# Seven products for eight in six k-tiles: half of the last gating projection and half of the output projection of a decoder layer

## The chip, the core and the metric

The kernel runs on one core of one Trainium2 chip. A core has a matrix engine (TensorE, PE in the profile, with its weight loads as PEld), a vector engine (VectorE, DVE), a scalar engine (ScalarE, ACT), GpSimd (POOL), a queue that issues transfers (SyncE, SP), sixteen DMA engines, a working memory of 128 partitions (SBUF) and eight accumulation banks for the matrix engine (PSUM). Each engine works through its own queue of instructions; they wait for each other with semaphores. The metric is the time of one execution on the device, in microseconds; less is better. A time is the median of several executions.

## What is computed

One decoder layer for 256 tokens of width 2048. Three branches (a convolution module A, a gated spatial mixer B, sparse attention C) are computed from one normed input, each is projected to the model width and multiplied by a gate; the sum goes through the output projection and a norm, and then a feed-forward network follows. The part that matters here:

```python
h = rms_norm(x, norm_mix_pre[l])
proj = h @ w_in[l]
a_in, b_in, q, kv, nsa_g, merge_g = jnp.split(proj, splits, axis=-1)
y_a = conformer_conv(a_in, ...)             # ends in  h @ w_a_out
y_b = chunked_spatial_gating(b_in, ...)     # ends in  (u * f) @ w_b_out
y_c = native_sparse_attention(q, kv, ...)   # ends in  o @ w_c_out
g_a, g_b, g_c = jnp.split(jax.nn.sigmoid(merge_g), 3, axis=-1)
mixed = (g_a * y_a + g_b * y_b + g_c * y_c) @ w_o[l]
x = x + rms_norm(mixed, norm_mix_post[l])
```

The three gates are 3 x 2048 columns of `proj`. The gate of branch C is the last 2048 of them.

## The kernel before

**Numbers in two parts.** All large products are made in a shortened float32 format. Each operand is split into a high part and a rest (`whi`, `wlo` for weights; `hT[:, k, 0]` and `hT[:, k, 1]` for the input), and a product of 128x128 by 128x512 is made of three matmuls: high by high, high by rest, rest by high (`mm_t`, L191 to L194). Inputs are cut into k-tiles of 128 rows; 2048 rows are 16 k-tiles. Tokens come in two halves of 128 (`t` = 0, 1; H1 and H2 in the change), output columns in blocks of 512.

**Weights.** `fetch` issues a transfer of one weight piece (128x1024, 512 KB) into a ring of five buffers (`wraw`). ScalarE copies the high part into one of four `whi` buffers (L143), VectorE subtracts it for the rest into one of four `wlo` buffers (L144). A buffer of a ring is taken again when its last reader has finished; for `whi` and `wlo` the last reader is a matmul. `piece` (L129) does this for one piece, `granule` for two.

**PSUM.** Four banks form a ring called "acc", the other four a ring called "bg" (`bank`). A bank is taken again when its last reader has finished.

**The gating.** `branch(bi, act_of)` (L867) runs once per branch, and inside it over four blocks of 512 columns. For a block it makes the gate product `pg` from `hT` and `wt_g` over 16 k-tiles, in two banks (one per half of the tokens), takes tanh on ScalarE (L883, 128x256 each, four per block), makes the branch's own product `py` from its result (8 k-tiles) and `wt_p`, and then VectorE multiplies (L908) and adds into `mac` (L911). For branch C, `mix_gen` then transposes the four finished k-tiles of `mac` on TensorE (L921), writes the high part into `mh` (L922) and the rest into `ml` (L923).

**Work in the background.** `bg` is a list of generators; `pump` takes steps from it between the products, so that attention, sums and transposes lie among them. A planner then sets the order of the instructions on each engine by priorities; `tc.high_priority` raises them, and `tc.issue_after` and `in_line` fix an order.

**The output projection.** `mm_o` multiplies `mh`, `ml` with `wt_o` by blocks of 512 columns (cb), pairs of k-tiles (p) and halves of the tokens; `done_o` squares the result for the norm (L960) and multiplies it by the gain row `rw` (L962, tile rnmp). The last pieces are held back (`HELD`) so that the second half of the tokens can be interleaved with the next norm's transposes (`enter2`, L989).

**Seven for eight, already in use.** The down projection of the feed-forward network (`Pair`, L1236 on) takes its k-tiles in part by pairs. Two k-tiles, two halves of the tokens and two blocks of columns make eight products; with sums and differences of the activations and of the weights prepared beforehand, seven products and a few additions at the end give the same result (the scheme of Strassen and Winograd, with four of the products accumulated in banks of their own: p1, p5, p6, p7). `quad` prepares the weights of such a pair: four subtractions of 512 columns and the split of seven half-pieces, in an order fixed by `fixed`, where each instruction of VectorE or ScalarE follows the one before in its list (L980 is the line where all of these are issued). `combine` adds the side banks up at the end.

Of the kernel before, what the change touches and what calls it, by code (L numbers as in the profile page):

```python
# [23 lines left out]
R = mybir.dt.float32r  # L25
# [13 lines left out]
PLAIN = [*range(22, 33), 21, 10, *range(33, NFT)]  # L39
BA, BB, BC, BG = 2100, 2200, 2200, 2500  # L40
# [14 lines left out]
def block(ctx: ExitStack, tc: tile.TileContext, x, xf, fp, cst, rows, sgw, w1, w2, wf_a, wt_bv, wf_bu, wf_c,  # L55
          wt_vs, wf_q, wt_g, wt_p, wt_o, wf_up, wt_dn, wt_dq, out):
# [134 lines left out]
    def mm_t(ps, xh, xl, hi, lo, first, last):  # L191
        PE.matmul(ps, lhsT=xh, rhs=hi, start=first, stop=False)  # L192
        PE.matmul(ps, lhsT=xh, rhs=lo, start=False, stop=False)  # L193
        return PE.matmul(ps, lhsT=xl, rhs=hi, start=False, stop=last).ins  # L194
# [634 lines left out]

    def attn():  # L830
# [27 lines left out]


# [4 lines left out]
    def branch(bi, act_of):  # L864

        for cb in range(4):
# [20 lines left out]
            for q in range(2):  # L887
                hs = granule(wt_p[(bi * 4 + cb) * 2 + q])
                if cb == 0 and q == 0:
                    until("BAC"[bi])  # L890
                    if bi == 2:
                        mix["h"] = s16(P1, [128, KT, T], R, "mh")
                        mix["l"] = s16(P1, [128, KT, T], R, "ml")
                act = act_of()
                for k in range(4 * q, 4 * q + 4):
                    hi, lo = hs[(k % 4) // 2]
                    c = slice((k % 2) * 512, (k % 2) * 512 + 512)
                    for t in range(2):
                        ts = slice(t * 128, t * 128 + 128)
                        mm_t(py[t], act[:, k, 0, ts], act[:, k, 1, ts], hi[:, c], lo[:, c], k == 0, k == 7)  # L900
                if q == 0:
                    pump(BUDGET)
# [13 lines left out]
    def mix_gen(cb):  # L916

        for k in range(4 * cb, 4 * cb + 4):
            pt = bank([128, T], f"pm{k}")
            for t in range(2):  # L920
                PE.transpose(pt[:, t * 128:t * 128 + 128], mac[:, t, k * 128:k * 128 + 128], ident)  # L921
            S.activation(mix["h"][:, k], pt, AF.Copy, scale=0.5)  # L922
            V.scalar_tensor_tensor(mix["l"][:, k], pt, 0.5, mix["h"][:, k].bitcast(F32), op0=ALU.mult,  # L923
                                   op1=ALU.subtract)
            yield 500

# [4 lines left out]
    mh, ml = mix["h"], mix["l"]  # L931

# [12 lines left out]
    def wo(cb, p):  # L945
        return wt_o[cb * 4 + p // 2][:, (p % 2) * 1024:(p % 2) * 1024 + 1024]

    def mm_o(cb, t, p, hl, halves=(0, 1)):
        if p == 0 and 0 in halves:
            po[cb, t] = PS.tile([128, 512], F32, tag="acc", name=f"po{cb}_{t}")  # L950
# [21 lines left out]
    seq = {}  # L972

    def fixed(eng, op, *args, **kw):

        with ExitStack() as order:
            order.enter_context(tc.high_priority())
            for ins in seq.get(eng, ()):
                order.enter_context(tc.issue_after(ins))
            seq[eng] = [op(*args, **kw).ins]  # L980

    def order_of(last):
        seq[V] = seq[S] = list(last)

# [19 lines left out]
    for cb in range(3):  # L1004
        for p in range(8):
            if (cb, p) in HELD:
                continue
            hl = piece(wo(cb, p), 1024)
            for t in range(2):
                mm_o(cb, t, p, hl)  # L1010
            pump(1e6)
        if cb < 2:
            for t in range(2):
                done_o(cb, t)
# [146 lines left out]
    H1, H2 = slice(0, 128), slice(128, T)  # L1161

# [49 lines left out]

# [17 lines left out]
    def high(hi, x):  # L1230
        fixed(S, S.activation, hi, x, AF.Copy)

    def rest(lo, x, hi):
        fixed(V, V.tensor_sub, lo, x, hi.bitcast(F32))

    def weights(src, into=None):  # L1236
        raw = fetch(src, 1024)
        hi, lo = (into[:, 0], into[:, 1]) if into is not None else ring(raw.name)
        high(hi, raw)
        rest(lo, raw, hi)  # L1240
        return hi, lo

    def ring(name):
        return [P0.tile([128, 1024], R, tag=tag, bufs=4, name=f"{tag}{name}") for tag in ("whi", "wlo")]

    class Pair:
        def __init__(self, p):
            self.p = p
            main = [PS.tile([128, 512], F32, tag="acc", name=f"pd{p}a{i}") for i in range(4)]
            side = [bank([128, 512], f"pd{p}b{i}") for i in range(4)]  # L1250
            if not p:
                main, side = side, main
            self.c = [main[0:2], main[2:4]]
            self.p1, self.p5, self.p6, self.p7 = side
            self.begun, self.left = set(), {}

        def mm(self, bank, a, w, last=False):

            first = id(bank) not in self.begun
            self.begun.add(id(bank))  # L1260
            for j, (x, y) in enumerate(((0, 0), (0, 1), (1, 0))):
                ins = PE.matmul(bank, lhsT=a[x], rhs=w[y], start=first and j == 0, stop=last and j == 2).ins  # L1262
            return ins

        def plain(self, i):

            hi, lo = weights(wt_dn[self.p, i])
            for n in range(2):
                c = slice(n * 512, n * 512 + 512)
                for t in range(2):  # L1270
                    in_line(self.mm, self.c[t][n], g2(PLAIN[i], (H1, H2)[t]), (hi[:, c], lo[:, c]),
                            self.p == 0 and i == len(PLAIN) - 1)

        def quad(self, n):
# [3 lines left out]
            last = n == len(PAIRS) - 1  # L1278
            L, U = slice(0, 512), slice(512, 1024)
# [3 lines left out]
            nm = f"q{self.p}_{j}"  # L1283
            tt = scratch()
            (hb, lb), (ha, la), (ht, lt), (h4, l4) = (ring(nm + x) for x in "bat4")
            high(hb, b)
            fixed(V, V.tensor_sub, tt[:, L], b[:, L], a[:, U])
            fixed(V, V.tensor_sub, a[:, U], a[:, U], a[:, L])
            high(ha, a)
            rest(lb, b, hb)  # L1290
            fixed(V, V.tensor_sub, tt[:, U], b[:, L], a[:, U])
            high(ht, tt[:, 0:1024])
            rest(la, a, ha)
            fixed(V, V.tensor_sub, tt[:, 1024:], b[:, U], tt[:, U])
            high(h4[:, L], tt[:, 1024:])
            rest(lt, tt[:, 0:1024], ht)
            rest(l4[:, L], tt[:, 1024:], h4[:, L])
            src = (se, sf)[j // 5]
            s1, s2, s4 = ((src[:, 0, j % 5, i], src[:, 1, j % 5, i]) for i in range(3))
            for bank_, act, (h, l), c in (  # L1300
                    (self.c[0][1], s4, (hb, lb), L), (self.c[0][0], g2(k1, H1), (hb, lb), U),
                    (self.p1, g2(k0, H1), (ha, la), L), (self.p5, s1, (ha, la), U),
                    (self.p7, g2(k0, H2), (ht, lt), L), (self.p6, s2, (ht, lt), U),
                    (self.c[1][0], g2(k1, H2), (h4, l4), L)):
                side = any(bank_ is x for x in (self.p1, self.p5, self.p6, self.p7))
                in_line(self.mm, bank_, act, (h[:, c], l[:, c]), last and side)
# [4 lines left out]

        def combine(self):

            fixed(S, S.activation, self.at(0, 0), self.p1, AF.Copy)
            fixed(V, V.tensor_add, self.at(1, 0), self.p6, self.at(0, 0))
            fixed(V, V.tensor_add, self.at(0, 1), self.p5, self.at(1, 0))
            fixed(V, V.tensor_add, self.at(1, 1), self.p7, self.at(0, 1))
            fixed(V, V.tensor_add, self.at(1, 0), self.p7, self.at(1, 0))
# [85 lines left out]
def _layout(inp):  # L1404
# [75 lines left out]
    for qt in range(2):  # L1480
# [7 lines left out]

    return {
# [3 lines left out]
        "wf_c": feat(w_in, c_cols), "wt_vs": wt_vs, "wf_q": feat(w_in, q_cols), "wt_g": tok(w_in, g_cols),  # L1493
        "wt_p": wt_p, "wt_o": tok(g["w_o"][0], slice(None)), "wf_up": feat(g["w_up"][0], up_cols),
        "wt_dn": plain, "wt_dq": quads,
# [19 lines left out]
```

## Time and profile before

| | |
|---|---|
| time, median of 3 runs | 1577.49 us (1576.95 to 1578.68) |
| the profiled execution, its time | 1577.03 us |
| its span, first to last instruction | 1575.3 us |
| TensorE busy | 1563.5 us (99%) |
| VectorE busy | 1230.8 us (78%) |
| ScalarE busy | 892.2 us (57%) |
| read from memory | 301.23 MB |
| granted TensorE clock, mean | 0.999 |

The page of a profile gives the busy time of each engine, a picture of the span in forty slices, the chain of work that ended last, and the costliest groups of instructions. A group's row has the line, the engine, the operation, the tile written and the tiles read, the shape, the count, then the busy time and the mean duration of one in ns, and last the idle time of the engine just before these instructions and what ended it. Durations of neighbours on an engine overlap a little; what one more instruction costs is the distance from one start to the next.

### The profile page before, as it was taken

Reading aid. Unit: us, or ns where it says so; the run is one execution under the profiler, and the core shown is the slowest. Engines: PE = TensorE matmul, PEld = TensorE weight load, DVE = VectorE, ACT = ScalarE, POOL = GpSimd, SP = SyncE. Lnnn points to the kernel's source line nnn. Section 1 sums busy time; section 2 is a strip of 40 time slices with the busy share of each in tenths; the row PEclk is TensorE's granted clock in tenths of the full one; section 3 lists DMA queues with packets and bytes.
Section 4 is the critical chain, followed back from the end, with each engine's and each line's share of the span. In section 5 each row is a group of like instructions: output and inputs, shape, how many; then the busy total and the mean of one; then the engine's idle time right before and its main releaser. Section 6 shows DMA issues by size and latency. Waiting matters only on the chain.

```text
span 1575.3 us, 22341 instructions
## 1 busy us (share of the span) xinstructions
PE 1563.5 (99%) x8173; PEld 1328.8 (84%) x8173; DVE 1230.8 (78%) x2114; ACT 892.2 (57%) x1442; POOL 17.7 (1%) x46
## 2 busy tenths in 40 slices
PE   9999999999999999999999999999999999999997
PEld 7888889888888787788888888888888888888886
DVE  7799999857866555465557988888777777799997
ACT  7544554447646675644456666565555555556563
POOL 1000020000000000000000000000000000000000
PEclk9999999999999999999999999999999999999999
DMA  9565566665765545555774666665666666766671
GB/s 376 183 193 180 190 176 211 193 196 179 235 200 155 161 136 172 160 188 186 243 250 150 204 192 187 192 187 187 188 188 192 190 191 190 232 208 214 209 283 70
DMA packets 85438, 307.94 MB, mean 195 GB/s; under 512 B 9808, under 2 KB 10832, under 8 KB 84304
## 3 DMA queue, kind: packets, MB, share of 16 engines
q1 hardware_dynamic: 83952, 301.91, 60.5%
q0 software_dynamic: 944, 4.19, 0.8%
q8 instruction: 64, 1.05, 0.3%
q10 hardware_dynamic: 432, 0.41, 0.1%
q14 instruction: 46, 0.38, 0.1%
HBM read 301.23 MB, written 4.19 MB: 194 GB/s over the span
## 4 chain that ended last, share of the span: by engine, by line
PE 98%; DVE 1%; DMA 0%; issue 0%; ACT 0%; DVEq 0%; SPq 0%; ACTq 0%
PE ps L172 29%; PE ps L179 15%; PE pg L193 6%; PE pg L192 6%; PE pg L194 6%; PE pd0b L1262 5%; PE pd1a L1262 5%; PE py L193 3%; PE py L194 3%; PE py L192 3%; PE po L192 2%; PE po L193 2%; PE po L194 2%; PE pd0a L1262 2%; PE pd1b L1262 1%; PE pv L192 1%
## 5 line engine op out<-in xcount | busy, mean ns | idle before, releaser
L144 DVE TENSOR_TENSOR wlo<-wraw,whi 128x1024 fp32r<-128x1024 f32 x440 | 536.5, 1222 | 170.7 <-ACT whi L143 164.1
L143 ACT ACTIVATE whi<-wraw 128x1024 fp32r<-128x1024 f32 x440 | 461.2, 1053 | 243.0 <-PE pg L194 97.1
L172 PE MATMUL ps<-h2T,whi 128*128 128x512 f32 x1360 | 325.0, 391 | 0.0
L172 PEld LDWEIGHTS ps<-h2T,whi 128*128 128x128 f32 x1360 | 249.9, 188 | 48.1
L179 PEld LDWEIGHTS ps<-h2T,wlo 128*128 128x128 f32 x1360 | 174.6, 191 | 6.7
L179 PE MATMUL ps<-h2T,wlo 128*128 128x256 f32 x1360 | 176.6, 283 | 0.0
L172 PE MATMUL ps<-hT,whi 128*128 128x512 f32 x640 | 157.4, 392 | 0.0
L214 ACT ACTIVATE t<-ps 128x256 f32<-128x256 f32 x125 | 47.7, 382 | 186.8 <-PE ps L172 186.3
L194 PE MATMUL pg<-whi,hT 128*128 128x512 f32 x384 | 151.1, 393 | 0.0
L193 PE MATMUL pg<-wlo,hT 128*128 128x512 f32 x384 | 150.8, 393 | 0.0
L192 PE MATMUL pg<-whi,hT 128*128 128x512 f32 x384 | 147.7, 393 | 0.0
L172 PEld LDWEIGHTS ps<-hT,whi 128*128 128x128 f32 x640 | 116.1, 189 | 21.2
L215 DVE TENSOR_TENSOR t<-ps,t 128x256 f32<-128x256 f32 x125 | 53.1, 426 | 70.3 <-ACT t L214 70.0
L475 DVE SCALAR_TENSOR_TENSOR cv<-hb,fps,cv 128x256 f32<-128x256 f32 x240 | 106.4, 491 | 0.2 <-ACT cv L471 0.2
L179 PEld LDWEIGHTS ps<-hT,wlo 128*128 128x128 f32 x640 | 84.7, 191 | 4.7
L179 PE MATMUL ps<-hT,wlo 128*128 128x256 f32 x640 | 86.8, 283 | 0.0
L193 PEld LDWEIGHTS pg<-wlo,hT 128*128 128x128 f32 x384 | 72.2, 188 | 16.1 <-issue 1.1
L194 PEld LDWEIGHTS pg<-whi,hT 128*128 128x128 f32 x384 | 72.2, 188 | 15.1 <-issue 0.7
L192 PEld LDWEIGHTS pg<-whi,hT 128*128 128x128 f32 x384 | 71.8, 188 | 14.7 <-issue 0.3
L980 DVE TENSOR_TENSOR wlowraw<-wraw,whiwraw 128x1024 fp32r<-128x1024 f32 x44 | 53.1, 1223 | 13.0 <-ACT whiwraw L980 12.2
L980 ACT ACTIVATE whiwraw<-wraw 128x1024 fp32r<-128x1024 f32 x44 | 46.3, 1056 | 17.9 <-PE pd0b L1262 8.0
L1192 ACT ACTIVATE fa<-fs,fps 128x256 f32<-128x256 f32 x88 | 52.3, 595 | 1.2 <-DVE fs L217 0.9
(1020 smaller groups left out, 2464.1 us busy)
## 6 DMA issues: line engine op xcount, KB each, us to landing
wraw<-in_wf_up_dram SPq DMA_DIRECT2D x176, 512.0 KB, 4.3
wraw<-in_wt_g_dram SPq DMA_DIRECT2D x96, 512.0 KB, 4.3
wraw<-in_wt_p_dram SPq DMA_DIRECT2D x48, 512.0 KB, 4.1
wraw<-in_wt_dn_dram SPq DMA_DIRECT2D x48, 512.0 KB, 4.5
wraw<-in_wf_a_dram SPq DMA_DIRECT2D x32, 512.0 KB, 4.1
wraw<-in_wt_o_dram SPq DMA_DIRECT2D x32, 512.0 KB, 4.7
wraw<-in_wt_dq_dram SPq DMA_DIRECT2D x20, 512.0 KB, 4.6
qa<-in_wt_dq_dram SPq DMA_DIRECT2D x20, 512.0 KB, 4.1
```

The lines of the kernel that those rows point to most:

```text
L143: S.activation(hi[:, :n], raw[:, :n], AF.Copy)
L144: V.tensor_sub(lo[:, :n], raw[:, :n], hi[:, :n].bitcast(F32))
L172: ins = PE.matmul(ps[:, :, ts], lhsT=ws[k // 8][0][:, c:c + 128], rhs=mov[:, k, :, ts], start=(k == 0 and not t), stop=(k == n - 1), skip_ ...
L179: ins = PE.matmul(ps[:, 1, ts], lhsT=ws[k // 8][1][:, c:c + 128], rhs=mov[:, k, 0, ts], start=False, stop=False, skip_group_check=True).ins
L192: PE.matmul(ps, lhsT=xh, rhs=hi, start=first, stop=False)
L193: PE.matmul(ps, lhsT=xh, rhs=lo, start=False, stop=False)
L194: return PE.matmul(ps, lhsT=xl, rhs=hi, start=False, stop=last).ins
L215: V.tensor_add(t1 if rb is not None else dst, ps[:, 0], t1)
L475: V.scalar_tensor_tensor(ca[:, j], hb[:, j, k:k + T], w(j, k), ca[:, j], op0=ALU.mult, op1=ALU.add)
L980: seq[eng] = [op(*args, **kw).ins]
L1192: S.activation(a, s, AF.Identity, bias=fps[:, C_FB + f:C_FB + f + 1], scale=w[2])
L1262: ins = PE.matmul(bank, lhsT=a[x], rhs=w[y], start=first and j == 0, stop=last and j == 2).ins
```

## The change

Two products are taken in another way: the gate of branch C for its second 1024 columns (blocks 2 and 3 at once), and the output projection for its first 1024 columns (blocks 0 and 1 at once). In both, the k-tiles 0 to 5 are taken as three pairs with seven products each, and the k-tiles 6 to 15 plainly. Each of the two uses all eight banks: four for the sums, four for p1, p5, p6 and p7. The classes of the down projection are moved up and made general (`Seven`; `Pair` becomes a child of it and does the same as before).

- `input_sums` makes the sums of `hT` for the three pairs, among the attention steps; `mix_gen` now transposes two k-tiles into one bank and makes the sums of the mix for the first three pairs.
- `branch` runs only blocks 0 and 1 for branch C. Then the half projection with 1024 columns follows (`in_sevens`), then the four tanhs (now 128x512), then `py` for block 2 (banks pyc) and block 3 (banks pyd).
- The output projection's first half follows with `in_sevens` again, in banks poa and pob; its results are added up in `y1`, and then block 2 goes on as before.
- The weights of the two halves lie in memory in the order in which they are used (wt_gp, wt_gq, wt_op, wt_oq). The number of transfers and their sizes stay.

Cut to its core:

```diff
+NG, REST = 3, list(range(6, KT))
...
+    def sums4(a0, a1, dst, nm):
+        p, q = q1(f"sp{nm}"), q1(f"sq{nm}")
+        V.tensor_add(p[:, H1], a0[:, H2], a1[:, H2])
+        V.tensor_sub(p[:, H2], p[:, H1], a0[:, H1])
+        V.tensor_sub(q[:, H1], a1[:, H1], p[:, H2])
+        V.tensor_sub(q[:, H2], a0[:, H1], a0[:, H2])
+        for i, x in enumerate((p, q)):
+            d = [dst[:, j, 2 * i:2 * i + 2].rearrange("p a b -> p (a b)") for j in range(2)]
+            S.activation(d[0], x, AF.Copy)
+            V.tensor_sub(d[1], x, d[0].bitcast(F32))
+    def input_sums(j):
+        a = [q1(f"ha{j}{i}") for i in range(2)]
+        for i in range(2):
+            V.tensor_add(a[i], hT[:, 2 * j + i, 0].bitcast(F32), hT[:, 2 * j + i, 1].bitcast(F32))
+        sums4(a[0], a[1], sh[:, j], f"h{j}")
+        yield 0
...
             yield from u.weights()
+            if n % 2 and n // 2 < NG:
+                yield from input_sums(n // 2)
...
+    class Seven:
...
+        def k_tiles(self, ws, act, last=False, t_first=False):
+            todo = [(k, w, t, n) for k, w in ws for n in range(2) for t in range(2)]
+            for k, (hi, lo), t, n in sorted(todo, key=lambda x: x[2]) if t_first else todo:
+                c = slice(n * 512, n * 512 + 512)
+                in_line(self.mm, self.c[t][n], act(k, (H1, H2)[t]), (hi[:, c], lo[:, c]), last)
...
+    def in_sevens(pr, plain, pairs, act, acts, tt, nm):
+        todo = [(k, weights(plain[REST.index(k)])) for k in REST[0:2]]
+        pr.k_tiles(todo, act, t_first=True)
+        rest_ = REST[2:]
+        for j in range(NG):
+            for _ in range((2, 2, 1)[j]):
+                k = rest_.pop(0)
+                pr.k_tiles([(k, weights(plain[REST.index(k)]))], act)
+            b, a = (fetch(pairs[j][:, x:x + 1024], 1024) for x in (0, 1024))
+            pr.seven(b, a, tt, acts(j), f"{nm}{j}", j == NG - 1)
+        for k in rest_:
+            w = weights(plain[REST.index(k)])
+            if k == rest_[-1]:
+                pr.combine()
+            pr.k_tiles([(k, w)], act, k == rest_[-1])
...
-        for cb in range(4):
+        for cb in range(2 if bi == 2 else 4):
...
+            if j < NG:
+                a = [q1(f"ma{j}{i}") for i in range(2)]
+                for i in range(2):
+                    S.activation(a[i], pt[:, i], AF.Copy, scale=0.5)
+                if j % 2 == 0:
+                    mix[j // 2] = s8([128, 2, 2, 4, 128], R, f"sm{j}")
+                sums4(a[0], a[1], mix[j // 2][:, j % 2], f"m{j}")
+                yield 1500
...
+    gates = s8([128, 2, 2, 512], F32, "gates")
+    tt = s8([128, 2048], F32, "tt")
+    pr = Seven([PS.tile([128, 512], F32, tag="acc", name=f"pga{i}") for i in range(4)],
+               [bank([128, 512], f"pgb{i}") for i in range(4)])
...
+    order_of(())
+    in_sevens(pr, wt_gp, wt_gq, hx, acts_h, tt, "g")
+    for n in range(2):
+        for t in range(2):
+            fixed(V, V.tensor_add, gates[:, t, n], pr.c[t][n], gates[:, t, n])
+            fixed(S, S.activation, gates[:, t, n], gates[:, t, n], AF.Tanh, scale=rh[:, t:t + 1])
+    pump(1e6)
+    Ct = Ct_box["t"]
+    for n in range(2):
+        cb = 2 + n
+        py = [bank([128, 512], f"pyc{t}") if n == 0 else PS.tile([128, 512], F32, tag="acc", name=f"pyd{t}")
+              for t in range(2)]
+        for k in range(8):
+            if k % 2 == 0:
+                hi, lo = weights(wt_p[(8 + cb) * 2 + k // 4][:, k % 4 * 512:k % 4 * 512 + 1024])
...
+        for t in range(2):
+            cc = slice(cb * 512, cb * 512 + 512)
+            with tc.high_priority(offset=int(PR)):
+                V.scalar_tensor_tensor(gates[:, t, n], gates[:, t, n], 1.0, py[t], op0=ALU.add, op1=ALU.mult)
+                V.tensor_add(mac[:, t, cc], mac[:, t, cc], gates[:, t, n])
+        bg.append(mix_gen(cb))
+        pump(1e6)
...
-    for cb in range(3):
-        for p in range(8):
-            if (cb, p) in HELD:
-                continue
-            hl = piece(wo(cb, p), 1024)
-            for t in range(2):
-                mm_o(cb, t, p, hl)
-            pump(1e6)
-        if cb < 2:
-            for t in range(2):
-                done_o(cb, t)
+    in_sevens(po2, wt_op, wt_oq, m2, acts_m, tt, "o")
+    for n in range(2):
+        for t in range(2):
+            r = po2.at(t, n)
+            fixed(V, V.tensor_add, r, po2.c[t][n], r)
+            S.activation(junk, r, AF.Square, accum_out=ss1[t][:, n:n + 1])
+            V.tensor_mul(r, r, rw[:, n * 512:n * 512 + 512])
+    for p in range(5):
+        hl = piece(wo(2, p), 1024)
+        for t in range(2):
+            in_line(mm_o, 2, t, p, hl)
```

`weights` fetches a piece and issues its high part and its rest through `fixed`; `seven` is the body of `quad` as it was, with its seven products in the order c01, c00, p1, p5, p7, p6, c10.

More of the change, by code (lines that the diff above doesn't have):

```diff
@@ L1228, in block @@
     order_of(())
[L1230 to L1246, printed above, removed]
+    class Pair(Seven):
         def __init__(self, p):
@@ L1250, in __init__ @@
             side = [bank([128, 512], f"pd{p}b{i}") for i in range(4)]
[L1251 to L1263, printed above, removed]
-        def plain(self, i):
[L1267 to L1272, printed above, removed]
+            super().__init__(*((main, side) if p else (side, main)))
+        def plain(self, i):
+            self.k_tiles([(PLAIN[i], weights(wt_dn[self.p, i]))], g2, self.p == 0 and i == len(PLAIN) - 1)
         def quad(self, n):
```

159 lines of the change are left out of this document (106 added, 53 removed).

## The prediction

> **What bounds the kernel now.** I read the page first (the span, the engines, the chain that ended last), then the busy times by stretch around the two projections, then TensorE, ScalarE and VectorE in order of time there, and last the stage that already uses such products. Of the page:
>
> ```profile
> span 1575.3 us, 22341 instructions
> ...
> PE 98%; DVE 1%; DMA 0%; issue 0%; ACT 0%; DVEq 0%; SPq 0%; ACTq 0%
> ...
> L144 DVE TENSOR_TENSOR wlo<-wraw,whi 128x1024 fp32r<-128x1024 f32 x440 | 536.5, 1222 | 170.7 <-ACT whi L143 164.1
> L143 ACT ACTIVATE whi<-wraw 128x1024 fp32r<-128x1024 f32 x440 | 461.2, 1053 | 243.0 <-PE pg L194 97.1
> ```
>
> TensorE is 98% of the chain. The weight pieces (L143 the high part, L144 the rest) wait for TensorE, not the other way round. By stretch, where the change lies:
>
> ```profile
> core 0: us, PE busy (x) PEld busy (x) DVE busy (x) ACT busy (x) POOL busy (x), PEclk, DMA share, GB/s
> ...
> 700.00:710.00 10.00, 10.00 (x45) 8.29 (x45) 4.39 (x4) 4.24 (x4) 0.00 (x0) 1.00 0.61 185
> ...
> 760.00:770.00 10.00, 10.00 (x50) 8.29 (x49) 5.43 (x8) 4.46 (x8) 0.00 (x0) 1.00 0.95 362
> ...
> sum 90.00, PE 90.00 PEld 74.57 DVE 50.18 ACT 41.75 POOL 1.08; mean PE 10.00 PEld 8.29 DVE 5.58 ACT 4.64 POOL 0.12
> ```
>
> Over 690 to 780 us TensorE has no gap at all, VectorE is busy 56% and ScalarE 46% of the time, and the granted clock is 1.00. So a matmul taken out here is worth its full distance to the next one, and every wait put in is paid in full. The distance, from TensorE in order of time (start, duration):
>
> ```profile
> 744.30 0.39 PE L192 MATMUL py<-whi,Ct 128*128 128x512 f32 x1
> ...
> 754.95 0.39 PE L194 MATMUL py<-whi,Ct 128*128 128x512 f32 x1
> ...
> 761.07 0.81 PE L921 MATMUL pm<-idn,mac 128*128 128x128 f32 x6
> 761.65 0.48 PE L194 MATMUL po<-whi,ml 128*128 128x512 f32 x1
> 761.96 0.39 PE L192 MATMUL po<-whi,mh 128*128 128x512 f32 x1
> ```
>
> From 744.30 to 754.95 lie 47 steps, 0.2266 us each; a duration of 0.39 is the time until the result can be read. After a block of transposes the next step takes 0.31 instead, 0.08 more.
>
> **The gain.** A pair of k-tiles needs eight products of three matmuls, now seven: three pairs in each of two projections, 18 matmuls of 128x512 less, 18 x 0.2266 = **-4.08**. The transposes stay 32, but in the built queue the changes between transposes and products fall from 141 to 137, two blocks less: -0.17.
>
> **Where it puts waits in.** ScalarE and VectorE work through their queues in order, and the changed program fixes much of that order. These rows give the prices: the first two fences are ScalarE in order of time, the third VectorE in the down projection, the fourth groups of instructions (busy, mean ns).
>
> ```profile
> 743.82 1.57 ACT L883 ACTIVATE mg<-pg,rh 128x256 f32<-128x256 f32 x4 [0.98 <-PE pg L194]
> 745.26 1.08 ACT L143 ACTIVATE whi<-wraw 128x1024 fp32r<-128x1024 f32 x1
> 747.22 1.06 ACT L143 ACTIVATE whi<-wraw 128x1024 fp32r<-128x1024 f32 x1 [0.88 <-PE py L194]
> ```
>
> ```profile
> 760.82 1.06 ACT L143 ACTIVATE whi<-wraw 128x1024 fp32r<-128x1024 f32 x1 [1.65 <-PE po L194]
> 761.78 0.64 ACT L922 ACTIVATE mh<-pm 128x256 fp32r<-128x256 f32 x2
> ```
>
> ```profile
> 1513.88 0.69 DVE L980 TENSOR_TENSOR qa<-qa 128x512 f32<-128x512 f32 x1
> 1514.49 1.22 DVE L980 TENSOR_TENSOR wloq_1b<-wraw,whiq_1b 128x1024 fp32r<-128x1024 f32 x1
> 1515.62 0.69 DVE L980 TENSOR_TENSOR fin<-wraw,qa 128x512 f32<-128x512 f32 x1
> ```
>
> ```profile
> L883 ACT ACTIVATE mg<-pg,rh 128x256 f32<-128x256 f32 x48 | 18.8, 471 | 9.2 <-PE pg L194 9.2
> ...
> L962 DVE TENSOR_TENSOR y<-po,rnmp 128x512 f32<-128x512 f32 x6 | 4.1, 684 | 0.0
> L960 ACT ACTIVATE junk<-po 128x512 bf16<-128x512 f32 x7 | 4.1, 585 | 8.8 <-PE po L194 8.8
> ...
> L1400 DVE SCALAR_TENSOR_TENSOR fin<-fin,rsyd,back 128x512 f32<-128x512 f32 x7 | 4.8, 748 | 0.1
> ...
> L1168 DVE TENSOR_TENSOR st<-fa,fa 128x128 f32<-128x128 f32 x10 | 2.9, 290 | 0.3
> ```
>
> Steps on one engine are shorter than durations: a high part 0.96 (760.82 to 761.78), a gate tanh (745.26 - 743.82) / 4 = 0.36, a 256-column copy about 0.3 (two end within 0.64), a 512-column subtraction 0.61, a 1024-column rest 1.13.
>
> *First wait, at the start of the half projection.* Its banks pga0 and pga1 are those of block 1's gates, and they are free only when the four tanhs (L883) have read them. Before, these stand ahead of the next high part (743.82, then 745.26). In the changed ScalarE queue they stand behind the high parts of the new k-tiles 6 to 9. The fourth of these takes the ring slot of the last y piece, so it waits for the last y matmul. From that matmul's start: 0.39 to its end, 0.96 for the high part, 0.3 for one copy of the sums, 0.36 and 0.47 for the two tanhs of pga0, 0.06 for hand-offs (estimate): 2.54, where 0.23 was the step: 2.31 lost. pga1 needs two more tanhs, 0.72 against three matmuls (0.68): 0.04. Behind the tanhs stand the last sums and the first piece of the first seven. **+2.4**; between 2.0 (no copy between) and 3.0 (the copy's input 0.6 late).
>
> *Second wait, in the first seven.* Transposes of k-tiles 4 to 7 stand in the TensorE queue ahead of k-tile 8. From their end TensorE has 24 matmuls and 0.08, so 5.75 until it wants the first rest of the seven. The other side, in order: 0.27 (a transpose's time to its end, from six taking 0.81 and five steps of 0.1), a high copy 0.6, its rest 0.75, two copies 0.7, four 128-column steps 0.8, two subtractions 1.2, two 256-column rests 0.66, the rest 1.22: 6.2. That is 0.4 late. Then each slot of the seven costs VectorE 0.61 + 1.13 = 1.74 where TensorE takes six matmuls, 1.36: twice 0.38 more. **+1.15**; between 0.4 and 2.
>
> *Third wait, before branch C's y of block 2.* The queue of ScalarE holds the four tanhs of the new gates (128x512) and only behind them the high part of y's first piece; the fourth tanh waits for the addition from pga3, and that for the last matmul of the projection. From its start: 0.39, the addition 0.68, a tanh of 512 columns, the high part 1.06, hand-offs 0.12. The tanh is not in the trace: between 0.36 and twice that; by the 585 ns of a 512-column read against a 256-column one I take 0.6. That is 2.85, less 0.23: 2.62. The second matmul wants the rest: 1.22 + 0.09 hand-offs - 0.23 = 1.08. **+3.7**; between 3.3 and 4.1. Behind that high part stand the next three pieces and y itself.
>
> **What I cost at nothing.** The other five sevens: a seven costs VectorE four subtractions and three and a half rests, 6.4, against 21 matmuls, 4.76; a plain k-tile returns 2.72 - 1.13 = 1.6, and the ring of four carries it over. The down projection does the same with twenty sevens, and TensorE's weight loads waited there for:
>
> ```profile
> PEld pd1a L1262 <- DVE wlowraw L980: 0.9, 1, 0.9
> PEld pd1b L1262 <- DVE wloq_4t L980: 0.4, 1, 0.4
> ```
>
> If the cover fails, 5 x 1.15 = 5.8. The hand-over to the output projection: the products of tokens 0 to 127 come first, 12 matmuls (2.7), and its banks wait only for two y steps of 0.75; its pieces stand ahead of these in both queues. Uncovered it would cost about 3. The input sums (some 2 us of VectorE for each of three pairs) lie among the attention steps, where VectorE has room, and the sums of the mix and the four more additions of 0.61 in stretches at 56%.
>
> The load of the gain row (rnmp) takes over a buffer that the second seven still reads. It moves from 636 us to right behind x2, three loads of 1 MB beside the weights instead of two:
>
> ```profile
> x<-in_x_dram POOLq DMA_DIRECT2D x2, 1024.0 KB, 9.1
> wraw<-in_wt_o_dram SPq DMA_DIRECT2D x3, 512.0 KB, 7.7
> ```
>
> Beside x2 a weight piece took 7.7 us to land, and TensorE did not wait. The first seven's pieces are issued before x2, so I take 0, with 2 as the upper end.
>
> **The sum.** -4.08 - 0.17 + 2.4 + 1.15 + 3.7 = **+3.0** on the profiled execution's 1577.0, which is 1580.0. The median of the runs, 1577.5, lies 0.5 above that execution, so **1580.5**. About 0.2%, 3.15 us, is what a measurement of this kernel can tell from no change: the forecast lies just inside that bound, and its own range, 1579.5 to 1581.6, on both sides of it.
>
> **The rivals.** *Fewer stalls.* VectorE keeps up in the first seven, and a wait or two is shorter: +0.3 to +2, 1577.8 to 1579.5. For it: 44% of VectorE is free; against it: the order is fixed, and the queued work depends on TensorE's own last results.
>
> *Faster.* The reads of the old banks and the new tanhs are covered, so that the weight pieces stay ahead in both hand-overs: then only the gain is left, 1573.3. It decides when the three waits together fall under 1.1 us. For it speaks the trace of before, where the same hand-over (743.82) costs TensorE nothing; against it the changed order of ScalarE's queue.
>
> *The clock.* Here TensorE would stand for 2.6 us, one matmul, then 1.1 us more. At the start of the kernel it is slow for some microseconds after standing idle:
>
> ```profile
> 1.42 4.02 PE L284 MATMUL warm<-wz 128*128 128x512 bf16 x9 [1.42 <-POOL wz L281]
> 5.48 2.95 PE L398 MATMUL pv<-swraw,hT 128*128 128x512 f32 x8
> 8.27 1.09 PE L398 MATMUL pv<-rwraw,hT 128*128 128x512 f32 x4
> 9.20 1.07 PE L192 MATMUL pv<-swraw,hT 128*128 128x512 f32 x4
> ```
>
> 21 matmuls from 1.42 to 9.20 take 7.8 us, at the later pace 4.8: once more the same would cost 3.0, 1583.5. Against it: 0.9 us waits in the down projection bring nothing of the kind. [...]
>
> *Weights late.* Either the sevens' deficit is not carried over or the three loads hold the pieces up: +2 to +6 more, 1582.5 to 1586.
>
> **How the numbers follow.** The forecast has 0.62, of it 0.32 within 0.2% and 0.30 above. Fewer stalls 0.12 (within), faster 0.08, the clock 0.08 and late weights 0.10 (slower). So faster 0.08, within 0.2% 0.44, slower 0.48. The range of 8 in 10 leaves out the faster case and the upper half of the late weights: 1577.0 to 1584.0.
>
> **What would show it.** TensorE idle in three places: before pga0, released by ScalarE's tanh of block 1, 2.4; in the first seven, three waits of about 0.4 for VectorE; before pyc0, released by ScalarE's high part, 2.6, then by VectorE's rest, 1.1; none in the output projection, and a granted clock of 1.00 throughout. 18 matmuls less. The forecast is wrong if the first or third wait is missing or the microseconds after them are slow (steps above 0.23 us).

## The result, and the profile after

The changed kernel takes 1585.4 us, the median of five runs (1583.48 to 1585.73), against 1576.95 before (1576.84 to 1578.68): a ratio of 1.0047, 95% interval 1.0035 to 1.0058. It is 8.4 us slower. The forecast was 1580.5 and its range ended at 1584.0. The profiled execution took 1585.73 us, 8.7 more than that of before.

The page of the changed kernel: span, busy times, and the chain that ended last.

```profile
span 1584.0 us, 22431 instructions
...
PE 1565.5 (99%) x8155; PEld 1326.1 (84%) x8155; DVE 1275.7 (81%) x2192; ACT 907.1 (57%) x1462; POOL 17.8 (1%) x46
...
PE 50%; DVE 2%; DMA 1%; issue 0%; ACT 0%; DVEq 0%; ACTq 0%
```

The 18 matmuls are gone (8155 for 8173), and yet TensorE counts as busy 2 us longer: what is left runs slower somewhere. The shares of the chain add up to 53%, so it is followed only part of the way back. A DMA stands in it with 1% and VectorE with 2%, where the chain of before had 0% and 1%.

What TensorE waited for between 600 and 900 us (total, times, longest, in us; the kernel before has no such row there):

```profile
PE pga L930 <- ACT mg L1011: 2.5, 1, 2.5
PE pyc L196 <- ACT whiwraw L895: 2.5, 1, 2.5
PE pyc L197 <- DVE wlowraw L895: 0.7, 1, 0.7
PE pga L930 <- DVE wlog0b L895: 0.2, 1, 0.2
```

These are the forecast's first wait, the two halves of its third, and the start of its second. Idle time is counted from the end of the last matmul, so the loss is better read from starts. TensorE in order of time, at the first wait, in the first seven, and at the third wait (start, duration):

```profile
687.65 0.39 PE L198 MATMUL py<-whi,Ct 128*128 128x512 f32 x1
690.54 0.50 PE L930 MATMUL pga<-whiwraw,hT 128*128 128x512 f32 x1 [2.50 <-ACT mg L1011]
690.88 0.40 PE L930 MATMUL pga<-wlowraw,hT 128*128 128x512 f32 x1
...
702.52 0.40 PE L930 MATMUL pga<-whig0b,sh 128*128 128x512 f32 x1
703.08 0.50 PE L930 MATMUL pga<-wlog0b,sh 128*128 128x512 f32 x1 [0.16 <-DVE wlog0b L895]
703.42 0.39 PE L930 MATMUL pga<-whig0b,sh 128*128 128x512 f32 x1
...
734.18 0.39 PE L930 MATMUL pga<-whiwraw,hT 128*128 128x512 f32 x1
737.05 0.55 PE L196 MATMUL pyc<-whiwraw,Ct 128*128 128x512 f32 x1 [2.49 <-ACT whiwraw L895]
738.31 0.80 PE L197 MATMUL pyc<-wlowraw,Ct 128*128 128x512 f32 x1 [0.71 <-DVE wlowraw L895]
738.90 0.63 PE L198 MATMUL pyc<-whiwraw,Ct 128*128 128x512 f32 x1
739.33 0.63 PE L196 MATMUL pyc<-whiwraw,Ct 128*128 128x512 f32 x1
```

A step is 0.23. The first wait took 2.89 for one step, and 0.11 more behind it: 2.8 lost. In the first seven 0.56 and 0.34 for two steps, and the same again, smaller, at the rests of the next two slots: 1.2 together. The third took 2.87 and 1.26 for two steps: 3.7. So far this is the forecast. But from 738.9 on a step takes 0.43, nearly twice 0.23. The stretches around it (length; busy time and count of each engine; the granted clock is the third column from the end):

```profile
737.20:737.40 0.20, 0.20 (x1) 0.04 (x1) 0.20 (x1) 0.20 (x1) 0.00 (x0) 0.93 0.00 0
737.40:737.60 0.20, 0.20 (x1) 0.00 (x0) 0.20 (x1) 0.20 (x1) 0.00 (x0) 0.50 0.00 0
738.30:744.00 5.70, 5.69 (x13) 4.46 (x14) 3.36 (x3) 2.13 (x3) 0.00 (x0) 0.50 0.71 213
744.00:744.20 0.20, 0.20 (x2) 0.17 (x1) 0.00 (x0) 0.20 (x1) 0.00 (x0) 0.51 0.66 225
744.20:744.40 0.20, 0.20 (x3) 0.16 (x2) 0.00 (x0) 0.20 (x1) 0.00 (x0) 1.00 0.50 205
```

The granted clock is 0.50 from about 737.4 to 744.2, 6.8 us. TensorE works in 5.9 of them at half speed, so 2.9 us are lost. The mean clock of the five runs is 0.995 or 0.996, against 0.998 or 0.999 before; 3.4 us at half speed lower a mean over 1580 us by 0.0011. (The clock is 0.50 too at the end of both traces, where TensorE has no more work: for 4.7 us in the kernel before, from 1570.6 on, and for 6.9 us in the changed one, from 1577.1 on. Alone these make means of 0.9985 and 0.998.)

The rest of the loss lies far from the change, in the second half of the down projection. Weight loads of TensorE from 1440 us on (before: 0.9 and 0.4, quoted in the prediction):

```profile
PEld pd1a L930 <- DVE wlowraw L895: 2.6, 3, 1.0
PEld pd1b L930 <- DVE wloq_2t L895: 0.5, 1, 0.5
PEld pd1b L930 <- DVE wloq_1t L895: 0.5, 1, 0.5
PEld pd1b L930 <- DVE wloq_4t L895: 0.4, 1, 0.4
PEld pd1b L930 <- DVE wloq_1a L895: 0.2, 1, 0.2
PEld pd1b L930 <- DVE wloq_2a L895: 0.2, 1, 0.2
```

Together 4.4 for 1.3. Nothing in the forecast has a term for this.

### The profile page after: what moved, and what is told of

It is laid out like the page before. It is cut to its first block, busy times and chain, and to the rows that moved or that the text cites. A ratio compares the mean times of both kernels' runs of the same rounds, so it can differ in the third digit from the quotient of the medians.

```text
span 1584.0 us, 22431 instructions
## 1 busy us (share of the span) xinstructions
PE 1565.5 (99%) x8155; PEld 1326.1 (84%) x8155; DVE 1275.7 (81%) x2192; ACT 907.1 (57%) x1462; POOL 17.8 (1%) x46
## 4 chain that ended last, share of the span: by engine, by line
PE 50%; DVE 2%; DMA 1%; issue 0%; ACT 0%; DVEq 0%; ACTq 0%
PE ps L176 20%; PE ps L183 10%; PE pd0b L930 5%; PE pd1a L930 4%; PE poa L930 2%; PE pd0a L930 2%; PE po L196 1%; PE po L198 1%; PE po L197 1%; PE pd1b L930 1%; DMA wraw<-in_wt_dn_dram 1%; PE pob L930 1%; DVE wlowraw L895 0%; DVE fin L895 0%; PE pu L1239 0%
## 5 line engine op out<-in xcount | busy, mean ns | idle before, releaser
L148 DVE TENSOR_TENSOR wlo<-wraw,whi 128x1024 fp32r<-128x1024 f32 x400 | 486.7, 1219 | 116.0 <-ACT whi L147 109.5
L147 ACT ACTIVATE whi<-wraw 128x1024 fp32r<-128x1024 f32 x400 | 419.0, 1053 | 187.3 <-PE pg L198 78.4
L198 PE MATMUL pg<-whi,hT 128*128 128x512 f32 x320 | 125.8, 393 | 0.0
L197 PE MATMUL pg<-wlo,hT 128*128 128x512 f32 x320 | 125.8, 393 | 0.0
L196 PE MATMUL pg<-whi,hT 128*128 128x512 f32 x320 | 122.2, 393 | 0.0
L895 DVE TENSOR_TENSOR wlowraw<-wraw,whiwraw 128x1024 fp32r<-128x1024 f32 x72 | 87.0, 1224 | 33.6 <-ACT whiwraw L895 32.5
L895 ACT ACTIVATE whiwraw<-wraw 128x1024 fp32r<-128x1024 f32 x72 | 75.4, 1056 | 43.6 <-PE pyc L198 9.0
L197 PEld LDWEIGHTS pg<-wlo,hT 128*128 128x128 f32 x320 | 60.1, 188 | 13.7 <-issue 1.1
L198 PEld LDWEIGHTS pg<-whi,hT 128*128 128x128 f32 x320 | 60.1, 188 | 12.7 <-issue 0.7
L196 PEld LDWEIGHTS pg<-whi,hT 128*128 128x128 f32 x320 | 59.8, 188 | 12.4 <-issue 0.3
```

The source lines that it names most:

```text
L147: S.activation(hi[:, :n], raw[:, :n], AF.Copy)
L148: V.tensor_sub(lo[:, :n], raw[:, :n], hi[:, :n].bitcast(F32))
```

## The experiments

Edits are shown against the changed kernel, if nothing else is said. All times stand beside runs of the kernel before on the same chip, median 1576.7 to 1576.9.

### Is it the stand-still that lowers the clock?

```diff
+        if n == 0:
+            for i in range(10):
+                in_line(lambda: PE.matmul(py[1], lhsT=Ct[:, 0, 0, H1], rhs=Ct[:, 0:2, 0], start=True, stop=True).ins)
         for k in range(8):
             if k % 2 == 0:
                 hi, lo = weights(wt_p...)
```

> Ten more matmuls of 128x512 (2.3 us of work whose results are thrown away: they go to the bank of pyc1, which its own first matmul clears) stand on TensorE between the last matmul of the half projection and the first of branch C's y, so the wait for ScalarE's high part is filled with work and no other instruction moves. If the halved clock behind the third wait comes from the stand-still (theory: clock), the first y matmul starts no later than in the changed kernel, the granted clock stays at 1.00 from 730 to 750 us and the time falls by the 3.4 us that the slow stretch cost: 1582.0. If the clock falls for another reason (rival), the slow stretch of 6.8 us stays and the time is that of the changed kernel, 1585.4. If the second stand-still of 0.7 to 1.0 us behind the first y matmul is enough, the stretch stays too. The matmuls themselves cost nothing if the high part is still what ends the wait.

1582.44 us (1580.54 to 1584.3, five runs), ratio 1.0036 [1.0022, 1.0049]. TensorE in order of time with the filling (L1103):

```profile
734.01 0.39 PE L930 MATMUL pga<-whiwraw,hT 128*128 128x512 f32 x1
734.24 2.43 PE L1103 MATMUL pyc<-Ct 128*128 128x512 f32 x10
736.89 0.50 PE L196 MATMUL pyc<-whiwraw,Ct 128*128 128x512 f32 x1 [0.22 <-ACT whiwraw L895]
738.15 0.50 PE L197 MATMUL pyc<-wlowraw,Ct 128*128 128x512 f32 x1 [0.76 <-DVE wlowraw L895]
738.49 0.40 PE L198 MATMUL pyc<-whiwraw,Ct 128*128 128x512 f32 x1
738.73 0.40 PE L196 MATMUL pyc<-whiwraw,Ct 128*128 128x512 f32 x1
```

The first y matmul stands 2.88 us behind the last gate matmul, as without the filling (2.87), and the second wait of 0.76 is still there. But the steps behind it are 0.24, the granted clock is 1.00 from 680 to 800 us, and this execution has a mean clock of 0.999. The other four runs have 0.997 or 0.998, all six of the changed kernel so far 0.995 or 0.996. So it is the stand-still of the third wait that lowers the clock here, and the 0.76 us alone did not. Useless matmuls make the kernel some 3 us faster.

### The third wait taken away

```diff
     in_sevens(pr, wt_gp, wt_gq, hx, acts_h, tt, "g")
+    early = [y_piece(2, 0), y_piece(2, 2)]
     for n in range(2):
         for t in range(2):
             fixed(V, V.tensor_add, gates[:, t, n], pr.c[t][n], gates[:, t, n])
...
             if k % 2 == 0:
-                hi, lo = weights(wt_p...)
+                hi, lo = early.pop(0) if early else y_piece(cb, k)
```

> The high parts and rests of branch C's first two y pieces of block 2 are put ahead of the four additions and four tanhs of the new gates in ScalarE's and VectorE's queues. Theory (third wait and its clock): TensorE has no wait before pyc0 (2.6 and 1.0 us less) and the clock does not fall (3.4 less): 1585.4 - 3.6 - 3.4 = 1578.4. Rival (the clock falls anyway): 1581.8. Second rival (the wait moves to the tanhs: y's own step or the next pieces come late): something of 1 to 3 us comes back before pyd or the output projection, 1579.5 to 1581.5.

1577.94 us (1576.37 to 1579.62, eleven runs), ratio 1.0006 [0.9997, 1.0015]: 7.5 below the changed kernel, about what the theory had (7.0; it took 3.4 for the clock, of which the trace gives 2.9). The wait before pyc0 is gone and nothing came back in its place. Its profiled execution (1579.62, the longest of the eleven) shows something else, at the first wait, where the changed kernel kept its clock (1.00 from 680 to 700 us):

```profile
686.98 0.39 PE L198 MATMUL py<-whi,Ct 128*128 128x512 f32 x1
689.87 0.50 PE L930 MATMUL pga<-whiwraw,hT 128*128 128x512 f32 x1 [2.50 <-ACT mg L1011]
```

The stretches of the same execution behind it (columns as above):

```profile
690.60:690.80 0.20, 0.20 (x3) 0.20 (x2) 0.20 (x1) 0.20 (x1) 0.00 (x0) 1.00 0.30 123
690.80:691.00 0.20, 0.20 (x3) 0.15 (x2) 0.20 (x2) 0.05 (x1) 0.00 (x0) 0.84 0.20 82
691.00:694.20 3.20, 3.20 (x9) 2.55 (x8) 2.58 (x8) 0.00 (x0) 0.00 (x0) 0.50 0.57 170
694.20:694.40 0.20, 0.20 (x2) 0.11 (x2) 0.00 (x0) 0.00 (x0) 0.00 (x0) 0.62 0.00 0
```

TensorE stood still for 2.66 us and then worked without a gap, and 1.1 us later, at 690.94, the clock fell to 0.50 for 3.4 us. One stand-still of 2.66 us was enough here; the same wait did not lower the clock in the changed kernel's profiles.

### Does the late end belong to the program?

> The changed kernel a second time, for what varies in it. The three waits of the hand-overs and the halved clock are in the program's order, so they stay within 0.3 us of 2.5, about 1, and 2.6 and 0.7; the slow stretch again is 5 to 8 us long. The waits of the down projection's second half (4.4 us of TensorE's weight loads in the first profile, 1.3 in that of the kernel before) stay near 4.4 if the change causes them, and go anywhere between 1 and 4.5 if they are the luck of the transfers.

> The kernel before a second time, for the same question: 1577 and 1.3 us of weight-load waits in the down projection's second half if these belong to the program; over 2.5 us of them, and a time up to 2 us longer, if they come and go with the transfers.

The kernel before: 1576.71, weight-load waits 0.9 and 0.4 again. The changed kernel: 1583.13, 2.6 below its first profile. The waits of 2.5 us and the halved clock are in the same places; the end is as before:

```profile
PEld pd1a L930 <- DVE wlowraw L895: 0.9, 1, 0.9
PEld pd1b L930 <- DVE wloq_4t L895: 0.4, 1, 0.4
```

So the late end is not in the order of the instructions; it comes and goes. What differs are two loads of 1 MB (back, the block's input for the last addition), which go out together ahead of weight pieces. Transfers between 1490 and 1530 us (count, size, median us from issue to landing), first the execution of 1585.73, then that of 1583.13:

```profile
back<-spill SPq DMA_DIRECT2D x2, 1024.0 KB, 8.7
wraw<-in_wt_dq_dram SPq DMA_DIRECT2D x3, 512.0 KB, 7.8
```

```profile
wraw<-in_wt_dq_dram SPq DMA_DIRECT2D x4, 512.0 KB, 5.4
back<-spill SPq DMA_DIRECT2D x2, 1024.0 KB, 6.1
```

### All three waits taken away

```diff
-    pr = Seven([PS.tile(... name=f"pga{i}") for i in range(4)], [bank(... f"pgb{i}") for i in range(4)])
+    pr = Seven([bank(... f"pga{i}") for i in range(4)], [PS.tile(... name=f"pgb{i}") for i in range(4)])
...
-            pump(BUDGET)
+            if (bi, cb) != (2, 1):
+                pump(BUDGET)
...
+    early = [y_piece(2, 0), y_piece(2, 2)]
...
+            if n and k == 4:
+                with tc.issue_after(pe_last[0]):
+                    pump(1e6)
```

The banks of the sums and the side banks change places (and pyc and pyd with them), so the first k-tiles don't wait for the tanhs of block 1. The transposes and sums of block 1 come behind the half projection, those of block 2 inside the last y.

> All the products of the change, without its three waits: the first k-tiles go to the four banks that no gate of branch C's block 1 occupies (the two groups of four banks change places), the transposes and sums of block 1 come after the half projection and those of block 2 in the middle of the last y, and the first two y pieces of block 2 are made before the new gates' additions and tanhs. Theory (the loss is the three waits, 7.2 us, and the clock behind the third, 2.9): TensorE has no wait from 680 to 800 us, a granted clock of 1.00 throughout, and the gain of 4.2 is left whole: 1576.8 - 4.2 = 1572.6 where the second half of the down projection is quiet, up to 2.6 more where it isn't; median 1573 to 1575. Rival (products by sevens cost more than their matmuls, in VectorE or in the transfers): waits for VectorE's rests of over 1 us in the other five sevens, 1576 or more.

1573.54 us (1572.46 to 1574.77, eleven runs), ratio 0.9977 [0.9969, 0.9986]: faster than both kernels. No wait of TensorE is left from 600 to 900 us. The lowest runs have the whole gain, and the runs spread over 2.3 us.

### The loads of back

> The same with one more edit: the two loads of 1 MB that bring the block's input back from memory in the second half of the down projection (back) go out after the second and the fourth seven instead of both behind the sixth. Theory (the wait of up to 2.6 us there comes from these two loads standing together ahead of weight pieces): TensorE's weight loads wait 1.3 us or less in all from 1440 us on, the times of the runs lie within 1 us of each other, 1572.3 to 1573.3. Rival (the transfers are slow for another reason): waits of 2.5 to 4 us in some runs, and the same spread as the kernel without this edit.

> The changed kernel with that edit alone (the two loads of back after the second and the fourth seven). Theory: the three waits and the clock stay, the waits of the down projection's second half fall from 3.9 to 4.4 (where they were bad) to 1.3, runs at 1582.5 to 1584.8 (the upper end where the first wait lowers the clock too, 1.7 us), median 1583.3 against 1585.4. Rival (not these loads): 1583 to 1586 as before the edit.

1573.76 us (1572.33 to 1574.77), ratio 0.9978 [0.9969, 0.9987], and 1584.38 us (1584.16 to 1585.39), ratio 1.0048 [1.0035, 1.0060]. Neither tests the theory, since the edit moved nothing. From SyncE's queue of the second kernel (start, duration):

```profile
1508.01 0.80 SPq L1488 DMA_DIRECT2D back<-spill  x2
```

Both loads still go out together, at the old place. Their buffer is one that TensorE reads until the fifth seven of that half (sf, L1333, has the same tag), so they can't be earlier, whatever the code says. They can be later:

```diff
-        if j == 5:
+        if j == 6:
             back = s16(P0, [128, 2, D], F32, "back")
-            for t in range(2):
+        if j in (6, 8):
+            t = (j - 6) // 2
+            with tc.issue_after(fetched[0]):
                 nc.sync.dma_start(back[:, t], spill[:, t])
```

> The changed kernel with the ten filling matmuls before branch C's y of block 2, and with the two loads of back taken apart: held behind the weight pieces of the seventh and of the ninth seven of the second half, where both stood behind the sixth. This takes away the clock behind the third wait and, if the theory holds, the late pieces at the end, and leaves the three waits and the gain: the prediction's sum by itself, +3.0. Theory: runs whose mean clock is that of the kernel before (0.998 or 0.999) take 1576.9 + 3.0 = 1579.9, within 0.6; runs at 0.997, where the first wait lowers the clock for 3.4 us, take 1.7 more, 1581.6; weight loads wait 1.3 us from 1440 us on. Rival (the end is late whatever the loads of back do): runs spread over 2.5 us and up to 1584 as with the filling alone.

1580.46 us (1580.16 to 1582.02, ten runs), ratio 1.0024 [1.0015, 1.0033]. Eight runs with a mean clock of 0.998 lie between 1580.16 and 1580.63, two with 0.997 at 1581.86 and 1582.02. The spread of 3.8 us of the filling alone falls into two levels 1.5 apart; 1.7 was expected for 3.4 us at half speed.

> The kernel without the three waits, with the two loads of back taken apart in the same way. Theory: the spread of 2.3 us of the kernel without this edit (1572.5 to 1574.8) shrinks to under 1, median 1572.5. Rival: the same median of 1573.5 and the same spread.

1572.4 us (1572.09 to 1572.87, six runs), ratio 0.9971 [0.9960, 0.9983]: the best version, 4.4 us below the kernel before. The loads now go out 19 us apart, and the spread of 2.3 us has shrunk to 0.8. From SyncE's queue:

```profile
1499.68 0.43 SPq L1499 DMA_DIRECT2D back<-spill  x1
1518.95 0.44 SPq L1499 DMA_DIRECT2D back<-spill  x1
```

They still take 7.9 us to land (median), but TensorE's weight loads wait no longer than in the quiet executions (0.9 and 0.4). The edit puts the loads later as well as apart, and which of the two helps was not tried. The two kernels without the waits ran on different chips; those with the filling ran on the same one. The stretches of this kernel where the change lies:

```profile
680.00:740.00 60.00, 60.00 (x273) 49.74 (x272) 52.26 (x76) 38.58 (x53) 0.00 (x0) 1.00 0.60 195
740.00:800.00 60.00, 60.00 (x272) 49.37 (x271) 52.31 (x65) 32.06 (x38) 1.64 (x3) 1.00 0.72 245
```

VectorE works 87% of this time (56% before, over 690 to 780), and TensorE has no gap.

> The kernel before with the two loads of back taken apart and nothing else, so that the edit at the end can be priced without the sevens. Theory: the kernel before seldom loses time there (two of some 30 runs lie 2 us above the rest), so its median stays within 0.4 us of 1576.8 and only the high runs go; then the whole difference to the kernel without waits (1572.4) is the sevens'. Rival: the edit itself saves time, 1576.2 or less, and part of the 4.4 us belongs to it.

1576.79 us (1576.44 to 1577.03, eleven runs), ratio 0.9999 [0.9990, 1.0008]: the edit at the end gains nothing by itself, so the 4.4 us are those of the sevens. Of 78 runs of the kernel before in the four comparisons, seven lie over 1578; with the loads apart none of eleven does, which with seven in 78 would also happen by chance about one time in three.

### One half of the change at a time

Here the output projection's half alone goes by sevens, with the gating of before (`branch` runs all four blocks for C again, no `input_sums`):

> The output projection's half alone by sevens, the gating as in the kernel before: 9 matmuls and two blocks of transposes less, 2.04 and 0.17 us. The prediction laid the first wait (2.4) to the gating's new k-tiles; if that is right this kernel has no wait at its hand-overs and takes 1576.8 - 2.2 = 1574.6. Rival: the wait comes from the sums of the mix (copies of 0.4 us and their like on ScalarE, which stand ahead of block 1's tanhs); then it appears here too, before the first gate matmul of branch C's block 2, 2.4 us, and the time is 1577.0, with 1.7 more where it lowers the clock: 1577 to 1579.

1579.35 us (1577.87 to 1581.7, eleven runs), ratio 1.0015 [1.0006, 1.0023], 2.4 above the kernel before. The four lowest runs, 1577.9 to 1578.1, lie about 1 above the rival's 1577.0 and far from the theory's 1574.6; the profiled one (1581.29) has the halved clock for 3.4 us and the late end besides. Its trace has one wait between 600 and 900 us:

```profile
PE pg L196 <- ACT mg L1008: 2.2, 1, 2.2
```

It is the first wait, in front of the gate of block 2, in a kernel without the half projection. And the gating's half alone, with the output projection of before (`mix_gen` without the sums):

> The half gating projection alone by sevens, the output projection as in the kernel before and so no sums of the mix: 9 matmuls less, 2.04 us, and some blocks of transposes. Theory (first and second wait come from the sums of the mix together with the sevens, the third from the gates alone): no wait before pga0 and none in the first seven, the third wait whole (2.6 and 1.0) with the halved clock behind it for two stretches of 3.4 us: 1576.9 - 2.1 + 3.6 + 2.9 = 1581.3, and up to 2.6 more where the end is late: 1581 to 1584. Rival (the first wait belongs to the half projection's k-tiles): 2.4 more, and a wait before pga0 in the trace.

1580.29 us (1578.35 to 1581.95, eleven runs), ratio 1.0021 [1.0012, 1.0030]. It waits before pyc alone, 2.5 and 0.8. The median lies below the theory's 1581 to 1584: in the profiled execution the slow clock lasted 3.4 us, not 6.8. ScalarE in order of time, first here, then in the changed kernel:

```profile
675.78 1.57 ACT L1011 ACTIVATE mg<-pg,rh 128x256 f32<-128x256 f32 x4 [1.23 <-PE pg L198]
677.22 1.08 ACT L147 ACTIVATE whi<-wraw 128x1024 fp32r<-128x1024 f32 x1
```

```profile
686.37 0.40 ACT L846 ACTIVATE sm<-spm 128x256 fp32r<-128x256 f32 x1
686.68 0.64 ACT L1060 ACTIVATE ma<-pm 128x256 f32<-128x256 f32 x2
...
688.40 1.06 ACT L895 ACTIVATE whiwraw<-wraw 128x1024 fp32r<-128x1024 f32 x1 [0.78 <-ACT sm L846]
689.37 0.40 ACT L846 ACTIVATE sm<-spm 128x256 fp32r<-128x256 f32 x1
689.67 1.55 ACT L1011 ACTIVATE mg<-pg,rh 128x256 f32<-128x256 f32 x4
```

Without the sums of the mix (ma, sm) the four tanhs run as soon as their gate is there, 14 us earlier, although the half projection's pieces stand in the queue as fixed as in the changed kernel. The second wait, in the first seven, is in neither half kernel: it needs the sums and the seven on VectorE at once. The mean clock is 0.996 to 0.999 over the runs of this kernel, so the third wait probably lowers it for two stretches of 3.4 us, for one, or not at all; only the profiled execution, with one, has a trace.

## Why the prediction was wrong

**The gain** (-4.25 with the transposes) was right. Without the waits it shows as -4.4.

**The three waits** were right in size: 2.8, 1.2 and 3.7 for 2.4, 1.15 and 3.7. The hand-offs in their sums (0.06, 0.12 and 0.09) were the author's estimates, which no row gives; in the changed kernel the first y matmul (737.05) starts 0.05 us after the end of its high part (735.96 and 1.04). With the gain that makes +3.5, where the forecast had +3.0, and the kernel with the filling and the loads apart measures it nearly alone: 1580.4, 3.6 above its runs of before.

**The cause of the first wait** was right in its last link and wrong in the one before. The tanhs did stand behind a high part that starts only after the last y matmul; in the changed kernel it starts 0.36 us after that matmul's end, which is the 0.4 by which the wait came out longer than forecast, and what it waited for in these 0.36 us stays open. But what put the tanhs there are the sums of the mix in `mix_gen`, not the new k-tiles of the half projection: the half kernel without the half projection has the wait, the one without the sums has not. Why the planner puts the tanhs behind the sums stays open.

**"A granted clock of 1.00 throughout"** is the first step that failed. The step took the stand-still of 2.6 us to cost its own length and no more; it was followed by 6.8 us at half clock, 2.9 us lost. The slow clock stood among the rivals, at this size (+3.0) and with a time of 1583.5 (the second profile took 1583.13), but with a chance of 0.08. The size was in part luck: it came from the slow start of the kernel, where 21 matmuls took 7.8 us at a granted clock that reads 1.00, and the same stand-still cost half as much in the trace of the kernel with the gating's half (3.4 us at half clock). The argument against it was that waits of 0.9 us in the down projection do no harm. That is still so (the granted clock of before is 1.00 up to 1570 us, and 0.76 did none behind the filling), and it said nothing of 2.6. Every run of the changed kernel has a lowered mean clock (0.995 or 0.996).

The clock did not answer the waits the same way each time: the slow stretches last 3.4 us in three traces (the early y pieces, each half of the change alone) and 6.8 us in the two profiles of the changed kernel, and the first wait of 2.5 us lowers the clock in the execution with the early y pieces and not in those of the changed kernel. No run shows what decides it.

**What was costed at nothing.** The other five sevens, the hand-over to the output projection, the input sums and the gain row cost nothing, as said: no wait of TensorE is left when the three are taken away. But the list went only through the places that the change touches. The transfers at the end are the second step that failed: 2.4 us between the changed kernel's two profiles (the starts of the same matmuls are 0.25 apart at 1445 us and 2.64 at the end). The late end is in five of the nine traces of kernels with sevens that load back in one go (slightly in a sixth), in neither trace of the kernel before. That the two loads of back have to do with it is shown by the kernels that take them apart: the runs' spread goes. Why these loads land late more often with the sevens is open: the issues stand in the same order and at nearly the same distances.

**The range** ended at 1584.0 because the upper half of the late weights was left out and no case joined two mishaps. The measured time is the sum as measured (+3.5), the clock (+2.9), and about 2 more, which the traces lay to the late end; in the runs at 0.995, which have no trace, it may be a clock that falls at the first wait too. The forecast's 0.5 for the median over the profiled execution came from three runs and was chance: the medians of before measured since are 1576.7 to 1576.95.

## What to carry to other kernels

A stand-still of TensorE of 2.5 us cost its length here and, in some executions, 1.7 or 2.9 us more at half clock (3.4 or 6.8 us at 0.50): cost it so in a forecast, and if it can't be removed, fill it with matmuls whose result nobody reads (1582.44 for 1585.4 us here). When a queue's order is fixed by hand, look for what else the planner fits in ahead of the instruction that frees the next bank; here sums that belong to a later stage held up the tanhs of the one before. Large loads that aren't urgent are best kept apart from each other and behind the pieces that are, as these two were in the best version.

## What was not expected of the hardware

The clock fell after TensorE was back at work: in the run with the early y pieces at 690.94 us, 1.1 us after the first matmul behind the wait, for 3.4 us of full work.

The same stand-still lowered the clock in some executions and not in others. The first wait is in seven traces. It was followed by 3.4 us at 0.50 in two, the early y pieces (2.50 us) and the output projection's half (2.23 us), and by a clock of 1.00 in the other five (2.5 us each). The third wait of 2.5 us is unfilled in four traces, and the clock fell in all of them. What decides is not shown.

The slow clock lasted 6.8 us in the two profiles of the changed kernel and in a third of the same order, with the edit that moved nothing, and 3.4 us in that of the gating's half, though all four have the second part of the third wait too (0.71, 0.61, 0.5 and 0.76 us). Why it lasted longer in three was not tried. At full clock the 0.76 us behind the filling lowered nothing.

Two loads of 1 MB behind one another landed after 6.1 us (median) or after 8.7, in executions of the same program.
